# Other PSUM banks for the inputs of layer 2, and a layer norm that goes block by block

## The chip, the cores and the metric

The kernel runs on one core of one Trainium2 chip. Its time is the device time of the program in microseconds, the median of several executions. Five engines of the core work beside each other, each on its own list of instructions, in the order of that list: TensorE (PE) multiplies matrices into PSUM banks, VectorE (DVE) and GpSimd (POOL) do elementwise work, ScalarE (ACT) does functions, copies and squares, and SyncE (SP) issues the transfers. They wait for each other through semaphores only.

## The reference

Two pre-norm residual layers over 2048 positions of width 1024, and a final RMS norm. Layer 1 is gated linear attention. Layer 2, where the change lies, is a convolution module:

```
h = rmsnorm(x, norm_w[1])
a, gl, z = split(h @ w_in, 3)
u = a * sigmoid(gl)
u = causal depthwise convolution of u, 31 taps, + dw_b
u = silu(layernorm(u, ln_w, ln_b))
x = x + (u * silu(z)) @ w_out
out = rmsnorm(x, final_norm_w)
```

## The kernel before

Everything is kept transposed: channels on the 128 partitions, positions along the free dimension. The 2048 positions are worked in two halves of 1024 (`hf` 0 and 1), each of two blocks of 512 (`b` 0 and 1), and the 1024 channels in eight tiles of 128 (`k` or `c`). Each float32 factor of a product is written as a sum of a high and a low part of a shorter type (`ah`, `al` for activations, `wh`, `wl` for weights; `split` makes the first, ScalarE the high part, VectorE the difference), and a product is three matmuls, `ah*wh + al*wh + ah*wl`. A column of 128 outputs over one block is so 8 x 3 = 24 matmuls of 128x512 into one bank of the pool `mm`, which has three banks.

Layer 2 of a half has these parts. `prep_x1` loads the input from a scratch in memory (`t<-x_scratch`), multiplies it with the norm's weight and the factor 1/rms of its position, and splits it. `in2` runs the projections as a list of units: `glu` units give `u` (TensorE, a sigmoid on ScalarE, a product on VectorE), gate units give `silu(z)`, which goes to memory (`sz_scratch`). While TensorE runs them, `conv` does the 31 taps of a channel tile on VectorE, with some of the taps on ScalarE and GpSimd (`convA`), in three chains B, A and C that end in the tile `d`, and GpSimd adds all `d` into `S1`. `layernorm` takes the mean with matmuls of `S1` and a matrix of ones (the bank `pm`, L693), centres each `d` (L700), squares and sums, takes 1/rms (`v4n` on VectorE, a power `r` on GpSimd), spreads it over the partitions with matmuls of `ident` (`broadcast`), multiplies (L727), does the Silu with weight and bias (L728), and multiplies with the gate read back (`b<-b,d`, L729). The first half writes this `y` to memory, the second splits it. `out2` multiplies `y` with the last weights, adds the input (`u` or `d`, L838), sums squares (`acc`) and scales with the final norm.

The order on each engine is set when the kernel is built. The functions hand out their instructions in an order with priorities (`tc.high_priority`, above all for what TensorE needs, and with offset 1000 for mean and scale), a list of background work (`bg`) is fed in by a credit of estimated times (`pump`), and a scheduler of the framework places each instruction by its own estimate of when its operands and its buffers are free. So the number of buffers in a pool changes the order too. PSUM has eight banks: before, `mm` three, `b` two (the chains of the convolution and squares), `m` three (means, 1/rms, broadcasts).

Of the kernel before, what the change touches and what calls it, by code (L numbers as in the profile page):

```python
# [13 lines left out]
P = 128  # L14
# [3 lines left out]
NB = 512  # L18
# [22 lines left out]
def kernel(  # L41
# [23 lines left out]
    small = ctx.enter_context(tc.tile_pool(name="small", bufs=4))  # L65
    ps_mm = ctx.enter_context(tc.tile_pool(name="ps_mm", bufs=3, space=bass.MemoryType.PSUM))
    ps_b = ctx.enter_context(tc.tile_pool(name="ps_b", bufs=2, space=bass.MemoryType.PSUM))
    ps_m = ctx.enter_context(tc.tile_pool(name="ps_m", bufs=3, space=bass.MemoryType.PSUM))


    def mm_bank():
# [3 lines left out]
        return ps_b.tile([P, NB], F32, name="pb")  # L75

    def m_bank():
        return ps_m.tile([P, NB], F32, name="pm")


    def cc(base, j, n=1):
# [98 lines left out]
            pe.matmul(ps[:, j * P:(j + 1) * P], r4[:, j:j + 1].to_broadcast([P, P]), ident, start=True, stop=True)  # L180
        return ps

    def factor(q, dst):

        ps = broadcast(rt[:, q:q + 4])
        act.activation(dst, ps, AF.Copy)
        return dst

    def split(src):
        hi, lo = act_pair()  # L190
        act.activation(hi, src, AF.Copy)
        dve.tensor_tensor(lo, src, hi.bitcast(F32), ALU.subtract)  # L192
        return hi, lo

    def prep_x1(hf, b, rb, temp):
        a = []
        t0 = hf * TH + b * NB
        for k in range(KT):
            xr = temp()
            sp.dma_start(out=xr, in_=x1d[k * P:(k + 1) * P, t0:t0 + NB])  # L200
            dve.scalar_tensor_tensor(xr, xr, cc(C_NW2, k), rb, ALU.mult, ALU.mult)
            a.append(split(xr))
        return a

    def accumulate(acc, sq, first, eng):
# [3 lines left out]

    l1 = ExitStack()
    s2 = l1.enter_context(tc.tile_pool(name="s2", bufs=1))
    l1p = l1.enter_context(tc.tile_pool(name="l1p", bufs=1))
    l1c = l1.enter_context(tc.tile_pool(name="l1c", bufs=1))
# [329 lines left out]
    for hf in range(2):  # L545
        a, EEs, g3s = nxt
        stage = []
        for h in range(HEADS):
            EEs = head(hf, h, a, EEs, g3s, stage)
        nxt = ([], [], [])  # L550
        if hf == 0:
            out1(hf, stage, lambda: start_block(1, 0, *nxt))
        else:
            a = []
            rbs = [factor(4 * b, t2("E")) for b in range(2)]
            out1(hf, stage, lambda: a.append(prep_x1(0, 0, rbs[0], lambda: t2("raw"))))
            a.append(prep_x1(0, 1, rbs[1], lambda: t2("raw")))
    l1.close()


# [2 lines left out]
    l2 = ctx  # L563
    s2 = l2.enter_context(tc.tile_pool(name="s2b", bufs=4, reuse_waits="tile"))
    l2p = l2.enter_context(tc.tile_pool(name="l2p", bufs=1, reuse_waits="tile"))

    def t2():
        return s2.tile([P, NB], F32, name="t2")
# [110 lines left out]
    def layernorm(hf, dst, S1, y_out):  # L679

        st = {}

        def view(t, b):
            return t[:, :, b * 256:(b + 1) * 256]

        def wide(t):
            return t.rearrange("p (s t) -> p s t", s=2)

        def mean(b):
            def fn():  # L690
                with tc.high_priority(offset=1000):
                    ps = m_bank()
                    pe.matmul(wide(ps), ones, view(S1[0], b), start=True, stop=True)  # L693
                st["mu", b] = ps
            return fn

        def centre(b, k):
            def fn():
                d = view(dst[k], b)
                dve.scalar_tensor_tensor(d, wide(st["mu", b]), -1.0 / D, d, ALU.mult, ALU.add)  # L700
                add = dve if k % 2 == 0 or (hf == 1 and b == 0) else pool
                if k == 0:
                    sq = view(S1[0], b)
                else:
                    sq = wide(b_bank() if add is dve else b2())
                act.activation(sq, d, AF.Square)
                if k > 0:
                    S2 = view(S1[0], b)
                    add.tensor_tensor(S2, S2, sq, ALU.add)
            return fn  # L710

        def scale(b):
            def fn():
                v4, r4 = small.tile([P, 4], F32, name="v4n"), small.tile([P, 4], F32, name="r4")
                with tc.high_priority(offset=1000):
                    S2 = view(S1[0], b)
                    inv_rms([S2[:, p, j * P:(j + 1) * P] for p in range(2) for j in range(2)], v4, r4)
                    st["rb", b] = broadcast(r4)
            return fn

        def norm(b, k):
            def fn():
                z = b2()
                sp.dma_start(out=z, in_=szd[hf, k * P:(k + 1) * P, b * NB:(b + 1) * NB])
                zv = wide(z)
                d = view(dst[k], b)
                dve.tensor_tensor(d, d, wide(st["rb", b]), ALU.mult)  # L727
                act.activation(d, d, AF.Silu, scale=cc(C_LNW, k), bias=cc(C_LNB, k))  # L728
                (pool if hf == 0 or k % 2 == 1 else dve).tensor_tensor(zv, zv, d, ALU.mult)  # L729
                y_out(k, b, z)  # L730
            return fn

        means = [(0.0, mean(b)) for b in range(2)]
        centres = [[(0.6 if k % 2 else 0.0, centre(b, k)) for k in range(KT)] for b in range(2)]
        scales = [(0.7, scale(b)) for b in range(2)]
        norms = [[(0.6, norm(b, k), (hf, k, b)) for k in range(KT)] for b in range(2)]
        if hf == 0:
            return means + centres[0] + centres[1] + scales + norms[0] + norms[1]
        both = [t for pair in zip(centres[1], norms[0]) for t in pair]
        return means + centres[0] + scales[:1] + both + scales[1:] + norms[1]  # L740

    def in2(hf, sched, a, y_out, ahead):
        dst, S1 = [], []
# [30 lines left out]
        for i, group in enumerate(groups):  # L774
            last = i == len(groups) - 1
            units = []
            if last and hf == 0:
                for b in range(2):
                    rbs.append(factor(8 + 4 * b, acc_tile()))
            for kind, j in group:  # L780
                w = next_unit((16 if kind == "u" else 24) + j)
                u = None
# [21 lines left out]
    def out2(hf, a):  # L804
        for b in range(2):
# [22 lines left out]
            def project(u, w, s):  # L828
                ss = slice(s * n, (s + 1) * n)
                for c in range(2):  # L830
# [7 lines left out]
                        dve.tensor_tensor(xr, ps, xr, ALU.add)  # L838
                    with tc.high_priority(offset=PRIO):
                        acc = accs[s][:, 0:n]  # L840
                        sq = acc if ch == 0 else b_bank()[:, 0:n]
                        act.activation(sq, xr, AF.Square)
                        if ch > 0:
                            dve.tensor_tensor(acc, acc, sq, ALU.add)
                    pump(4.4 / ns, 0.0)

            def finish(s):
                ss = slice(s * n, (s + 1) * n)
                kp = () if ns == 1 else (1, 3, 5) if s else (1, 3, 5, 7)
                with tc.high_priority(offset=1000 if ns > 1 else 0):  # L850
                    v4, r4 = small.tile([P, 4], F32, name="v4"), small.tile([P, 4], F32, name="r4f")
                    inv_rms(columns(accs[s], n // P), v4, r4, b_bank)
                    rb = broadcast(r4[:, 0:n // P], b_bank)
                    if kp:
                        rbs = t2()[:, 0:n]
                        act.activation(rbs, rb, AF.Copy)
# [31 lines left out]
    def load_y(b):  # L888
        res = []
        for k in range(KT):  # L890
            raw = t2()
            sp.dma_start(out=raw, in_=yd[k * P:(k + 1) * P, b * NB:(b + 1) * NB])
            res.append(split(raw))
        return res

    rbs = []
    nxt = []

    def ahead_a():
        with tc.high_priority(offset=PRIO):  # L900
            nxt.append(prep_x1(1, 0, rbs[0], t2))

    in2(0, SCHED[0], a, y_spill, ahead_a)
    with tc.high_priority(offset=PRIO):
        nxt.append(prep_x1(1, 1, rbs[1], t2))
    a, nxt = nxt, []

    def ahead_b():
# [82 lines left out]
```

## Time and profile before

| | |
|---|---|
| times of three runs | 1647.65, 1643.82, 1647.19 us |
| median | 1647.19 us |
| profiled execution | 1651.64 us, its span 1649.5 us |
| TensorE busy | 1603.0 us, 97% |
| VectorE busy | 950.6 us, 58% |
| ScalarE busy | 739.7 us, 45% |
| GpSimd busy | 888.7 us, 54% |
| mean granted clock of TensorE | 0.99 of full speed |

Times in the rows count from the span's start. A group's line gives its busy time, the mean of one instruction, and the idle time of its engine ahead of it with what ended that (`<-`). A row of the timeline gives the start, the length, the engine, the line, the operation with the tiles it writes and reads, and how many such instructions lie in a row; the length is that of the whole row. Successive instructions of an engine overlap a little: a VectorE operation shown as 0.68 us starts 0.60 us after one like it. Layer 1 ends near 890 us, the place between the halves of layer 2 lies near 1140 to 1180, and `out2` begins near 1450.

### The profile page before, as it was taken

What the parts mean: (1) busy time and instruction counts of PE and PEld (TensorE: products, weight loads), DVE (VectorE), ACT (ScalarE), POOL (GpSimd) and SP (SyncE); (2) the same over time, 40 slices, a digit from 0 to 9 for tenths busy, and PEclk for the clock granted to TensorE, in tenths of its full rate; (3) what the DMA queues carried; (4) which work ended last, traced back from release to release, by engine and by line L of the source; (5) the groups of instructions that cost most, each with busy time, mean ns of one, the idle gap of its engine ahead of it and who ended that gap; (6) DMA issues with size and microseconds to landing.
All of it is one profiled execution on the core that took longest, in us unless ns stands there. A gap on an engine that the chain in (4) does not pass through costs nothing.

```text
span 1649.5 us, 23586 instructions
## 1 busy us (share of the span) xinstructions
PE 1603.0 (97%) x9028; PEld 1407.4 (85%) x9028; DVE 950.6 (58%) x1495; ACT 739.7 (45%) x1244; POOL 888.7 (54%) x789
## 2 busy tenths in 40 slices
PE   8999999999999999999999999999999999989897
PEld 6989999998889898989888888887788888878796
DVE  7433232251334232323425699998888999887753
ACT  6655353252447352523333354544473545435532
POOL 5353333234664434342344599976488988356552
PEclk9999999999999999999999999999999999999898
DMA  6021211144511212122454111224254122653743
GB/s 193 27 83 53 64 53 57 58 130 145 154 58 52 83 34 81 36 75 73 128 172 135 51 52 52 78 71 133 89 172 155 50 77 77 200 170 109 272 144 121
DMA packets 80160, 165.68 MB, mean 100 GB/s; under 512 B 7760, under 2 KB 22608, under 8 KB 80048
## 3 DMA queue, kind: packets, MB, share of 16 engines
q1 hardware_dynamic: 80048, 164.19, 31.1%
q8 instruction: 70, 1.15, 0.3%
q14 instruction: 42, 0.34, 0.1%
HBM read 128.51 MB, written 35.65 MB: 100 GB/s over the span
## 4 chain that ended last, share of the span: by engine, by line
PE 80%; DVE 5%; DMA 5%; ACT 4%; issue 3%; POOL 2%; SPq 0%; POOLq 0%; DVEq 0%; ACTq 0%
PE mm L146 70%; PE pb L146 3%; DMA wr<-in_wall_dram 2%; DVE al L192 2%; PE pb L390 1%; PE pb L392 1%; PE pm L381 1%; DVE pb L637 1%; DMA raw<-x_scratch 1%; POOL wl L127 1%; PE pm L416 1%; PE pm L290 1%; DVE d L727 1%; DMA t<-x_scratch 1%; POOL acc L207 1%
## 5 line engine op out<-in xcount | busy, mean ns | idle before, releaser
L146 PE MATMUL mm<-ah,wh 128*128 128x512 f32 (+1 forms) x1600 | 595.1, 387 | 21.1 <-DVE u L838 5.6
L146 PE MATMUL mm<-al,wh 128*128 128x512 f32 (+1 forms) x1600 | 592.3, 385 | 0.0
L146 PE MATMUL mm<-ah,wl 128*128 128x512 f32 (+1 forms) x1600 | 590.6, 385 | 0.2 <-POOL wl L127 0.2
L127 POOL TENSOR_TENSOR wl<-wr,wh 128x1024 fp32r<-128x1024 f32 x140 | 341.2, 2451 | 230.9 <-ACT wh L126 229.9
L146 PEld LDWEIGHTS mm<-ah,wh 128*128 128x128 f32 x1600 | 301.8, 190 | 83.1 <-DVE u L838 6.1
L146 PEld LDWEIGHTS mm<-ah,wl 128*128 128x128 f32 x1600 | 301.2, 190 | 57.8 <-POOL wl L127 0.7
L146 PEld LDWEIGHTS mm<-al,wh 128*128 128x128 f32 x1600 | 301.9, 190 | 57.1 <-issue 0.2
L146 PE MATMUL mm<-wh,ah 128*128 128x256 f32 x896 | 259.3, 289 | 0.0
L146 PE MATMUL mm<-wh,al 128*128 128x256 f32 x896 | 254.7, 284 | 0.0
L146 PE MATMUL mm<-wl,ah 128*128 128x256 f32 x896 | 254.2, 284 | 0.0
L625 POOL TENSOR_TENSOR convA<-convA,prod 128x512 f32<-128x512 f32 x158 | 207.0, 1312 | 11.6 <-ACT prod L623 4.9
L126 ACT ACTIVATE wh<-wr 128x1024 fp32r<-128x1024 f32 x144 | 145.5, 1051 | 145.7 <-PE mm L146 108.8
L637 DVE SCALAR_TENSOR_TENSOR pb<-u,C,pb 128x512 f32<-128x512 f32 x274 | 199.5, 747 | 1.0
L637 DVE SCALAR_TENSOR_TENSOR pb<-u,dwc,pb 128x512 f32<-128x512 f32 x240 | 178.2, 748 | 1.3
L146 PEld LDWEIGHTS mm<-wl,ah 128*128 128x128 f32 x896 | 171.5, 191 | 0.4
L146 PEld LDWEIGHTS mm<-wh,ah 128*128 128x128 f32 x896 | 171.3, 191 | 0.4
L146 PEld LDWEIGHTS mm<-wh,al 128*128 128x128 f32 x896 | 171.3, 191 | 0.0
L623 ACT ACTIVATE prod<-u,C 128x512 f32<-128x512 f32 x158 | 112.7, 721 | 105.0 <-POOL convA L625 104.6
L399 DVE SCALAR_TENSOR_TENSOR S<-S,dec,pb 128x256 f32<-128x256 f32 x56 | 26.8, 478 | 95.4 <-PE pb L146 95.3
L403 POOL TENSOR_TENSOR ss<-ss,e 128x1 f32<-128x1 f32 x64 | 13.3, 208 | 124.5 <-ACT g L402 124.5
L528 DVE TENSOR_TENSOR Q<-mm,Q 128x512 f32<-128x512 f32 x32 | 22.0, 688 | 92.6 <-PE mm L146 78.6
L443 DVE SCALAR_TENSOR_TENSOR vl<-mm,r,vh 128x256 fp32r<-128x256 f32 x48 | 22.9, 483 | 89.3 <-ACT vh L442 89.2
(191 smaller groups left out, 2078.3 us busy)
## 6 DMA issues: line engine op xcount, KB each, us to landing
wr<-in_wall_dram SPq DMA_DIRECT2D x144, 512.0 KB, 4.1
raw<-in_xT_dram SPq DMA_DIRECT2D x32, 256.0 KB, 3.7
Q<-in_xP_dram SPq DMA_DIRECT2D x32, 256.0 KB, 3.2
x_scratch<-Q SPq DMA_DIRECT2D x32, 256.0 KB, 3.2
sz_scratch<-t SPq DMA_DIRECT2D x32, 256.0 KB, 2.3
b<-sz_scratch SPq DMA_DIRECT2D x32, 256.0 KB, 3.0
g_scratch<-st SPq DMA_DIRECT2D x48, 128.0 KB, 1.9
raw<-g_scratch SPq DMA_DIRECT2D x24, 256.0 KB, 3.7
```

Of the source, the lines that this page charges most:

```text
L126: act.activation(wh[:, ks, :], raw, AF.Copy)
L127: (dve if i < 2 else pool).tensor_tensor(wl[:, ks, :], raw, wh[:, ks, :].bitcast(F32), ALU.subtract)
L146: pe.matmul(ps, s, m, start=(i == 0), stop=(i == 3 * n - 1))
L192: dve.tensor_tensor(lo, src, hi.bitcast(F32), ALU.subtract)
L207: eng.tensor_tensor(acc, acc, sq, ALU.add)
L290: pe.matmul(ps, wgs[:, k, :], m, start=(n == 0), stop=(n == 15))
L399: dve.scalar_tensor_tensor(S[h], S[h], dec[:, j:j + 1], kv, ALU.mult, ALU.add)
L443: dve.scalar_tensor_tensor(vl, ps, rr, vh.bitcast(F32), ALU.mult, ALU.subtract)
L528: dve.tensor_tensor(xr, ps, xr, ALU.add)
L623: act.activation(p, src, AF.Copy, scale=w)
L625: pool.tensor_tensor(acc, acc, p, ALU.add)
L637: dve.scalar_tensor_tensor(dstm, src, w, ps, ALU.mult, ALU.add)
```

## The change

Three things are changed, all for layer 2.

First, the input of layer 2 is no longer multiplied in place: the product goes to a PSUM bank, and both halves of the split read it there. The bank comes from `m` for the first half (while layer 1 still has its pools) and from the new pool `x` for the second. The factor 1/rms is read by the product straight from the bank of its broadcast, made inside `prep_x1`; the copies of it to SBUF (`factor`) are gone. The `y` of the second half is put together in an `x` bank as well, by VectorE alone, and split from there; and `y` of the first half, read back from memory, is copied by ScalarE to an `x` bank beside the high part, and VectorE's low part reads that copy.

Second, in layer 2 the three spare banks, `m` before, become one bank `m` and two banks `x`. The squares of centring and of `out2` take `x` in place of `b`; the mean and 1/rms of the second half take `b`, those of the first half `m`; the final norm's broadcast takes `m`.

Third, the layer norm's list is dealt out anew: mean 0, centrings 0, mean 1, centrings 1, then scale 0, norms 0, scale 1, norms 1 for the first half (before: both means, all centrings, both scales, all norms), and the first half's means and scales lose their offset of 1000.

```diff
@@ pools of layer 2
+    banks["m"] = l2.enter_context(tc.tile_pool(name="ps_n", bufs=1, space=bass.MemoryType.PSUM))
+    banks["x"] = l2.enter_context(tc.tile_pool(name="ps_x", bufs=2, space=bass.MemoryType.PSUM))
@@ prep_x1
-    def prep_x1(hf, b, rb, temp):
+    def prep_x1(hf, b, temp, rb_bank, bank):
         a = []
         t0 = hf * TH + b * NB
+        q = hf * 8 + b * 4
+        rb = broadcast(rt[:, q:q + 4], rb_bank)
         for k in range(KT):
             xr = temp()
             sp.dma_start(out=xr, in_=x1d[k * P:(k + 1) * P, t0:t0 + NB])
-            dve.scalar_tensor_tensor(xr, xr, cc(C_NW2, k), rb, ALU.mult, ALU.mult)
-            a.append(split(xr))
+            t = bank()
+            dve.scalar_tensor_tensor(t, xr, cc(C_NW2, k), rb, ALU.mult, ALU.mult)
+            a.append(split(t))
@@ layernorm
+        bank, ahead = (m_bank, 0) if hf == 0 else (b_bank, 1000)
@@ mean
-                with tc.high_priority(offset=1000):
-                    ps = m_bank()
+                with tc.high_priority(offset=ahead):
+                    ps = bank()
@@ centre
-                    sq = wide(b_bank() if add is dve else b2())
+                    sq = wide(x_bank() if add is dve else b2())
@@ scale
-                    inv_rms([S2[:, p, j * P:(j + 1) * P] for p in range(2) for j in range(2)], v4, r4)
-                    st["rb", b] = broadcast(r4)
+                    inv_rms([S2[:, p, j * P:(j + 1) * P] for p in range(2) for j in range(2)], v4, r4, bank)
+                    st["rb", b] = broadcast(r4, bank)
@@ norm
-                act.activation(d, d, AF.Silu, scale=cc(C_LNW, k), bias=cc(C_LNB, k))
-                (pool if hf == 0 or k % 2 == 1 else dve).tensor_tensor(zv, zv, d, ALU.mult)
-                y_out(k, b, z)
+                y = d if hf == 0 else wide(x_bank())
+                act.activation(y, d, AF.Silu, scale=cc(C_LNW, k), bias=cc(C_LNB, k))
+                if hf == 0:
+                    pool.tensor_tensor(zv, zv, d, ALU.mult)
+                    y_out(k, b, z)
+                else:
+                    dve.tensor_tensor(y, zv, y, ALU.mult)
+                    y_out(k, b, y.rearrange("p s t -> p (s t)"))
@@ the lists
         if hf == 0:
-            return means + centres[0] + centres[1] + scales + norms[0] + norms[1]
+            return (means[:1] + centres[0] + means[1:] + centres[1]
+                    + scales[:1] + norms[0] + scales[1:] + norms[1])
         both = [t for pair in zip(centres[1], norms[0]) for t in pair]
-        return means + centres[0] + scales[:1] + both + scales[1:] + norms[1]
+        return means[:1] + centres[0] + scales[:1] + means[1:] + both + scales[1:] + norms[1]
@@ out2
-                        sq = acc if ch == 0 else b_bank()[:, 0:n]
+                        sq = acc if ch == 0 else x_bank()[:, 0:n]
-                    inv_rms(columns(accs[s], n // P), v4, r4, b_bank)
-                    rb = broadcast(r4[:, 0:n // P], b_bank)
+                    inv_rms(columns(accs[s], n // P), v4, r4, x_bank)
+                    rb = broadcast(r4[:, 0:n // P], m_bank)
@@ load_y
-            res.append(split(raw))
+            hi, lo = act_pair()
+            x = x_bank()
+            act.activation(hi, raw, AF.Copy)
+            act.activation(x, raw, AF.Copy)
+            dve.tensor_tensor(lo, x, hi.bitcast(F32), ALU.subtract)
+            res.append((hi, lo))
@@ the second half's input
-            nxt.append(prep_x1(1, 0, rbs[0], t2))
+            nxt.append(prep_x1(1, 0, t2, m_bank, x_bank))
-        nxt.append(prep_x1(1, 1, rbs[1], t2))
+        nxt.append(prep_x1(1, 1, t2, m_bank, x_bank))
```

The order of the instructions moves most at the place between the halves. On TensorE before, both means of the first half (`pm<-S,ones`) stand together, behind the first 72 projection matmuls of the second half:

```order
L146 MATMUL mm<-ah,wh 128x512
L146 MATMUL mm<-al,wh 128x512
L146 MATMUL mm<-ah,wl 128x512
L693 MATMUL pm<-S_9658,ones 128x512 x2
L146 MATMUL mm<-ah,wh 128x512
```

On TensorE now, the two means (counted here as one row, each needs the one bank `pm`) and the broadcast of the second half's factor (`ident,rt`) stand ahead of the last gate column of the first half:

```order
L150 MATMUL mm<-al,wh 128x512
L150 MATMUL mm<-ah,wl 128x512
L696 MATMUL pm<-S_9677,ones 128x512 x2
L184 MATMUL pm<-ident,rt 128x128 x4
L150 MATMUL mm<-ah,wh 128x512
```

They have moved 96 projection matmuls to the front. Where the means stood before, with the same number of projection matmuls ahead, TensorE now has the square sum and the broadcast of 1/rms of block 1 and the broadcast of the factor for the input's block 1:

```order
L150 MATMUL mm<-al,wh 128x512
L150 MATMUL mm<-ah,wl 128x512
L172 MATMUL pm<-ones,S_9677 128x1 x4
L184 MATMUL pm<-ident,r_11239 128x128 x4
L184 MATMUL pm<-ident,rt 128x128 x4
L150 MATMUL mm<-ah,wh 128x512
```

All three write the one bank, one after the other. On VectorE before, the products and splits of the second half's input (`t<-t,C,acc`, `al<-t,ah`) lie between the last taps of convolution 7 (`pb<-u,dwc,pb`, ended by `d<-pb,dwb,convB`), and the centrings of both blocks follow in one row:

```order
L637 SCALAR_TENSOR_TENSOR pb<-u,dwc,pb 128x512 x10
L201 SCALAR_TENSOR_TENSOR t_11338<-t_11338,C,acc 128x512
L637 SCALAR_TENSOR_TENSOR pb<-u,dwc,pb 128x512
L201 SCALAR_TENSOR_TENSOR t_11345<-t_11345,C,acc 128x512
L201 SCALAR_TENSOR_TENSOR t_11352<-t_11352,C,acc 128x512
L637 SCALAR_TENSOR_TENSOR pb<-u,dwc,pb 128x512
L192 TENSOR_TENSOR al<-t_11338,ah 128x512
L192 TENSOR_TENSOR al<-t_11345,ah 128x512
```

On VectorE now, convolution 7 ends first, then come centrings 0, centrings 1, and only then the products into the banks `px` and their splits:

```order
L639 SCALAR_TENSOR_TENSOR pb<-u,dwc,pb 128x512 x15
L655 SCALAR_TENSOR_TENSOR d<-pb,dwb_96,convB 128x512
L703 SCALAR_TENSOR_TENSOR d<-pm,d 128x2x256 x8
L712 TENSOR_TENSOR S_9677<-S_9677,px 128x2x256 x2
L703 SCALAR_TENSOR_TENSOR d<-pm,d 128x2x256 x8
L712 TENSOR_TENSOR S_9677<-S_9677,px 128x2x256
L203 SCALAR_TENSOR_TENSOR px<-t_11032,C,pm 128x512
L203 SCALAR_TENSOR_TENSOR px<-t_11040,C,pm 128x512
L190 TENSOR_TENSOR al<-px,ah 128x512 x2
```

The input has moved behind the layer norm's centrings. On ScalarE now, five high parts stand ahead of a copy that empties an `mm` bank (`t<-mm`), and further on 16 Silus, five high parts and a table load stand ahead of the next ones:

```order
L189 ACTIVATE ah<-px 128x512 x5
L776 ACTIVATE t_11121<-mm 128x512
L189 ACTIVATE ah<-px 128x512
L776 ACTIVATE t_11223<-mm 128x512
L732 ACTIVATE d<-d,C 128x2x256 x16
L189 ACTIVATE ah<-px 128x512 x5
L759 ACT_TABLE_LOAD
L759 ACTIVATE t_11474<-mm 128x512
```

Before, all but one of the 16 high parts and the copies came ahead of the table load and of the squares, and the Silus later. On SP now, the fifth load of block 1's input (`t_11393<-x_scratch`) stands behind the stores of `y` and the loads of the gate tiles:

```order
L887 DMA y_scratch<-b_11264 128x512
L727 DMA b_11282<-sz_scratch 128x512
L887 DMA y_scratch<-b_11270 128x512
L727 DMA b_11316<-sz_scratch 128x512
L201 DMA t_11393<-x_scratch 128x512
```

`b_11264`, `b_11270` and `b_11316` are the eleventh, twelfth and fifteenth of the 16 gate tiles; four buffers hold them. Before, these loads came ahead of all of them.

## Rows read from the trace of the kernel before

**Rows 1.** The page, busy time of the engines, and VectorE's 40 slices
```profile
PE 1603.0 (97%) x9028; PEld 1407.4 (85%) x9028; DVE 950.6 (58%) x1495; ACT 739.7 (45%) x1244; POOL 888.7 (54%) x789
...
DVE  7433232251334232323425699998888999887753
```

**Rows 2.** Waits of PE: total us, times, longest us
```profile
PE mm L146 <- DVE u L838: 5.6, 2, 4.1
...
PE mm L146 <- ACT t L750: 4.0, 3, 1.8
PE pb L168 <- DVE acc L844: 3.7, 2, 2.6
```

**Rows 3.** Timeline of PE: start, length, form, count, idle before
```profile
1143.04 0.39 PE L146 MATMUL mm<-ah,wl 128*128 128x512 f32 x1
1146.12 0.50 PE L146 MATMUL mm<-ah,wh 128*128 128x512 f32 x1 [2.70 <-ACT t L767]
...
1171.70 1.98 PE L693 MATMUL pm<-S,ones 128*128 128x512 f32 x4 [1.88 <-POOL S L660]
1175.49 0.50 PE L146 MATMUL mm<-ah,wh 128*128 128x512 f32 x1 [1.80 <-ACT t L750]
```

**Rows 4.** Timeline of DVE at the end of convolution 7
```profile
1142.59 2.85 DVE L192 TENSOR_TENSOR al<-t,ah 128x512 fp32r<-128x512 f32 x1
...
1149.46 0.68 DVE L192 TENSOR_TENSOR al<-t,ah 128x512 fp32r<-128x512 f32 x1
...
1151.33 7.87 DVE L637 SCALAR_TENSOR_TENSOR pb<-u,dwc,pb 128x512 f32<-128x512 f32 x10
...
1168.10 0.74 DVE L653 SCALAR_TENSOR_TENSOR d<-pb,dwb,convB 128x512 f32<-128x512 f32 x1
...
1177.08 9.65 DVE L700 SCALAR_TENSOR_TENSOR d<-pm,d 128x512 f32<-128x512 f32 x16
```

**Rows 5.** Timeline of POOL, the sum of convolution 7 to the y products
```profile
1132.74 1.43 POOL L625 TENSOR_TENSOR convA<-convA,prod 128x512 f32<-128x512 f32 x1 [0.27 <-ACT prod L623]
...
1142.07 5.60 POOL L127 TENSOR_TENSOR wl<-wr,wh 128x1024 fp32r<-128x1024 f32 x2
...
1168.92 2.72 POOL L660 TENSOR_TENSOR S<-S,d 128x1024 f32<-128x1024 f32 x1 [1.71 <-DVE d L653]
...
1198.19 1.02 POOL L170 TENSOR_TENSOR r<-v4n,mhalf 128x4 f32<-128x4 f32 x1 [1.47 <-DVE v4n L169]
...
1211.61 5.07 POOL L729 TENSOR_TENSOR b<-b,d 128x512 f32<-128x512 f32 x4
...
1220.73 1.30 POOL L729 TENSOR_TENSOR b<-b,d 128x512 f32<-128x512 f32 x1 [0.27 <-DMA b<-sz_scratch]
...
1223.23 2.55 POOL L729 TENSOR_TENSOR b<-b,d 128x512 f32<-128x512 f32 x2
...
1229.75 1.30 POOL L729 TENSOR_TENSOR b<-b,d 128x512 f32<-128x512 f32 x1 [1.12 <-DMA b<-sz_scratch]
```

**Rows 6.** Timeline of ACT: a high part, a copy, a table load, Silus
```profile
1145.47 0.60 ACT L767 ACTIVATE t<-mm 128x512 f32<-128x512 f32 x1 [2.13 <-DVE al L192]
...
1149.58 0.63 ACT L191 ACTIVATE ah<-t 128x512 fp32r<-128x512 f32 x1 [0.68 <-DVE t L201]
...
1173.54 1.28 ACT L750 ACT_TABLE_LOAD   x1
...
1210.18 5.06 ACT L728 ACTIVATE d<-d,C 128x512 f32<-128x512 f32 x7
```

**Rows 7.** Groups of DVE by line, 1128 to 1176 us
```profile
L192 DVE TENSOR_TENSOR al<-t,ah 128x512 fp32r<-128x512 f32 x15 | 14.7, 1001 | 0.0
```

**Rows 8.** A window behind PE's stand at 1146.12: us, busy, granted clock
```profile
1147.30:1150.60 3.30, 3.30 (x10) 0.50 0.93 250
```

**Rows 9.** DMA issues: count, KB each, us to landing
```profile
t<-x_scratch SPq DMA_DIRECT2D x16, 256.0 KB, 3.7
y_scratch<-b SPq DMA_DIRECT2D x16, 256.0 KB, 3.6
```

More of the change, by code (lines that the diff above doesn't have):

```diff
@@ L67 @@
     ps_b = ctx.enter_context(tc.tile_pool(name="ps_b", bufs=2, space=bass.MemoryType.PSUM))
-    ps_m = ctx.enter_context(tc.tile_pool(name="ps_m", bufs=3, space=bass.MemoryType.PSUM))
+    l1 = ExitStack()
+    banks = {"m": l1.enter_context(tc.tile_pool(name="ps_m", bufs=3, space=bass.MemoryType.PSUM))}
     def mm_bank():
@@ L77, in m_bank, with x_bank @@
     def m_bank():
-        return ps_m.tile([P, NB], F32, name="pm")
+        return banks["m"].tile([P, NB], F32, name="pm")
+    def x_bank():
+        return banks["x"].tile([P, NB], F32, name="px")
     def cc(base, j, n=1):
@@ L181, in broadcast @@
         return ps
[L183 to L187, printed above, removed]
     def split(src):
@@ L207, in accumulate @@
             eng.tensor_tensor(acc, acc, sq, ALU.add)
-    l1 = ExitStack()
     s2 = l1.enter_context(tc.tile_pool(name="s2", bufs=1))
@@ L554 @@
             a = []
-            rbs = [factor(4 * b, t2("E")) for b in range(2)]
-            out1(hf, stage, lambda: a.append(prep_x1(0, 0, rbs[0], lambda: t2("raw"))))
-            a.append(prep_x1(0, 1, rbs[1], lambda: t2("raw")))
+            out1(hf, stage, lambda: a.append(prep_x1(0, 0, lambda: t2("raw"), b_bank, m_bank)))
+            a.append(prep_x1(0, 1, lambda: t2("raw"), b_bank, m_bank))
     l1.close()
@@ L714, in fn @@
                 v4, r4 = small.tile([P, 4], F32, name="v4n"), small.tile([P, 4], F32, name="r4")
-                with tc.high_priority(offset=1000):
+                with tc.high_priority(offset=ahead):
                     S2 = view(S1[0], b)
-                    inv_rms([S2[:, p, j * P:(j + 1) * P] for p in range(2) for j in range(2)], v4, r4)
-                    st["rb", b] = broadcast(r4)
+                    inv_rms([S2[:, p, j * P:(j + 1) * P] for p in range(2) for j in range(2)], v4, r4, bank)
+                    st["rb", b] = broadcast(r4, bank)
             return fn
@@ L776, in in2 @@
             units = []
-            if last and hf == 0:
-                for b in range(2):
-                    rbs.append(factor(8 + 4 * b, acc_tile()))
             for kind, j in group:
@@ L892, in load_y @@
             sp.dma_start(out=raw, in_=yd[k * P:(k + 1) * P, b * NB:(b + 1) * NB])
-            res.append(split(raw))
+            hi, lo = act_pair()
[4 more added lines that the diff above has]
+            res.append((hi, lo))
         return res
-    rbs = []
     nxt = []
```

## The prediction, on record before the changed kernel ran

> **What bounds the kernel now.** I read the busy shares first. TensorE is busy 1603.0 of 1649.5 us, and VectorE, at 58% overall, is at eight or nine tenths in 13 slices of the last half [rows 1]. So nothing can be gained but TensorE's waits, and anything that makes TensorE stand is paid in full. The waits come second: TensorE's table of them is short, and in layer 2 nothing in it lasts over 4.1 us at a time [rows 2]. The change touches the place between the two halves of layer 2, so the timeline of TensorE there comes third [rows 3]: a stand of 2.70 us that ends at 1146.12, one of 1.88 us ahead of the two mean sums at 1171.70, and one of 1.80 us that ends at 1175.49. Beside it stand the rows of VectorE [rows 4], GpSimd [rows 5] and ScalarE [rows 6]. VectorE there does three things mixed: the last taps of convolution 7, and the products and splits of the second half's input, of which 15 splits take 14.7 us [rows 7]. Both centrings follow in one run of 16 (9.65 us, 0.60 each), since the two means lie in two of three `m` banks.
>
> **What the edits do singly.** 64 splits now read PSUM in place of SBUF. A split costs 0.68 us where GpSimd is quiet (1149.46) and 2.85 where it lasts beside the 5.60 us pair of weight splits (1142.59) [rows 4, 5]. Priced at the gap between the mean of 14.7/15 = 0.98 and 0.68, that is about 0.3 x 64 = 19 us of VectorE's time. The Trainium skill ("SBUF — State Buffer", Who interferes with whom) says that a VectorE instruction with two SBUF inputs contends with a GpSimd instruction that reads SBUF. These two rows agree; by the rule alone every split gets cheaper and the change is a gain, which is the first rival below. The eight y products that leave GpSimd and become VectorE's free 8 x 1.3 = 10 us of GpSimd [rows 5]. The 16 extra copies on ScalarE (0.63 each [rows 6], 10 us) lie on an engine that is 45% busy [rows 1]. None of these engines bounds the whole, so I count all of it as nothing and look for what now makes TensorE wait.
>
> **Place between the halves, first stand.** In the changed order mean 0, mean 1 and the broadcast of 1/rms for the second half's block 0 stand ahead of the last gate column of the first half, not 96 matmuls later, and all three use the single `m` bank. TensorE gets there at about 1143.3 (the last matmul in front starts at 1143.04) [rows 3].
> - Convolution 7: its GpSimd sum is there at 1132.74 + 1.43 = 1134.2, or 1132.8 without VectorE's products beside it [rows 5]. Then three VectorE operations at 0.66 to 0.75, 16 taps at 7.87/10 = 0.79, and the closing one, 0.74 [rows 4]: 2.1 + 12.6 + 0.74. The end is 1148.3 to 1149.7, I take 1148.5. The products that lay between them are gone, so this ends 20 us earlier than before (1168.84).
> - GpSimd's sum 2.7 [rows 5], mean 0 half of 1.98 [rows 3]: 1152.2. Eight centrings at 0.60: 1157.0. Only then is the bank free. Mean 1: 1158. Two square sums on VectorE that alternate with GpSimd's: about 1159.6; eight centrings: 1164.4; broadcast: 1165.2.
> - The input now goes through two `x` banks: two products (0.66 each), two splits (0.68 long, 0.61 apart), 0.2 for ScalarE's high part between them: 2.75 a pair. ScalarE has five high parts (0.63) ahead of the copy (0.60) that empties the oldest `mm` bank; all three are full. 1165.2 + 5.5 + 0.66 + 0.63 + 0.60 gives 1172.6; I take 1173.
>
> TensorE resumes at 1173 where it did at 1146.1: +27. The Trainium skill ("PSUM — Partial Sum Buffer", Engine vs sequencer instructions) says that matmuls start and complete in program order. The stand before the means at 1171.70 agrees: the projection behind them needed neither. By the rule no ready column can pass the means, whatever the other engines save.
>
> **Second stand.** From 1173: 96 matmuls at 0.227 = 21.8 (the column pace between 1146.12 and 1169.8 is that plus a slow stretch), about 2.5 lost behind the stand (in before, after a stand of 2.7, the granted clock was 0.50, 1.2 GHz in place of 2.4, for 3.3 us [rows 8], which loses half of that; this stand is ten times as long), 1.5 for broadcasts and sums: 1198.8. Here the changed order has block 1's square sum, the broadcast of its 1/rms and that of the input's 1/rms in a row, each on the one bank, and only then the next column.
> - 1/rms 0 is there at about 1189; the first normed product and Silu (0.6 and 5.06/7 = 0.72 [rows 6]) make the first y product start at 1190.8. Seven y products stand ahead of the second 1/rms on GpSimd. In before the y tiles' four buffers let a round of four go every 9.1 us (1211.61, 1220.73, 1229.75), and the seventh ended 14.2 after the first began [rows 5]. So 1205, power 1.0 [rows 5], broadcast 0.5, eight norms as long as the centrings, 4.9: 1211.4; broadcast, five products, high part: 1218.7.
> - The fifth tile of block 1's input is loaded by SP behind the stores of y and the reload for the fifteenth product, which needs the eleventh stored. The eleventh ends 1190.8 + 18.2 + 3.9 = 1212.9; store 3.6, load 3.7 [rows 9], two issues 0.5: 1220.7; product and high part: 1222.
> - ScalarE has 16 Silus, five high parts and a table load (1.28 [rows 6]) ahead of the copy (0.60) that frees an `mm` bank. That gives 1220.6 by the first path, 1224 by the second, and 1215.5 if the y products ran back to back.
>
> I take 1222, nearest to the rows of the y rounds. Both orders have the same matmuls ahead here, and before resumed at 1175.49 [rows 3]: +46.5. A second slow stretch costs 2; the next stand in the old table (about 1.5, of the two that make up the other 2.2 of `t` L750 [rows 2]) should go: **+47**, bounds +40 and +52. VectorE idles or norms during both stands, so the gain of the splits is spent there.
>
> **The rest.** VectorE starts the second half's convolution some 27 us later and TensorE is 47 later, so VectorE, full there before, has about 20 us in hand: the stand behind `u` L838 (4.1 [rows 2]) goes, with 1.5 of slow clock, -5.6. Against it, block 1's mean comes later in the last part, and the y products of the second half and the squares of the output share the two `x` banks: the final square sum stands behind 16 norm steps. No row of before shows that; the bounds are 0 and +14 (eight output products of about 0.75, a store and a load of 3.6 and 3.7), and I take +6, the nearest row being the wait for `acc`, 2.6 [rows 2], at each of the two square sums, and a little for the reload behind. At the change of layers the single `m` bank doesn't exist yet: 0 to -1. Sum: about 0.
>
> **Sum.** 1651.6 for the profiled run + 47 + 0 = 1698.6. That run is 4.4 above the median of the runs shown (1647.2), so the forecast is **1694**. Its own range is 1680 (+40 and no cost in the last part) to 1708 (+52, +14 and the -5.6).
>
> **Rivals.**
> 1. *The splits win.* From PSUM they no longer clash with GpSimd, everything is early, and the waits of [rows 2, 3] go: 4.1 + 2.7 + 1.9 + 1.8 + 1.5 and about 1 elsewhere, with two slow stretches of 1.5, about -16: 1631. It needs mean 0 ready when TensorE gets there, 1143.3 - 3.7 = 1139.6 for convolution 7's end. Against it: its GpSimd sum is not there before 1132.8 and 15.4 us of VectorE's chain follow. If that chain could be overlapped with the columns the case decides; I see no way. 0.06.
> 2. *Only the first stand.* If y products don't hold the second 1/rms, and the copies of the first columns come between the Silus, the second stand is below the three `mm` banks' cover: +27 + 2.5 - 3.3: 1647 + 26 = 1673. For it: scratch loads may run ahead. Against it: ScalarE's program has the 16 Silus in one row. 0.17.
> 3. *The last part is dearer.* The shared `x` banks cost the full 14 (+8 on my value) and the stand at `u` L838 stays with its slow clock (+5.6): 1708. The short cover of the last columns speaks for it, VectorE's lead against it. 0.12.
> 4. *Nothing moves:* the banks freed in the first stand make good later all that was lost: 1647. 0.05.
>
> My forecast has 0.60. A difference under 0.3% (5 us) can't be told from none with this kernel. Slower: 0.60 + 0.17 + 0.12 = 0.89, less 0.01 for the edges: 0.88; same 0.05, faster 0.07. The range must take in rival 2 in part: 1662 to 1712.
>
> **What would show it.** In the new trace, three stands of TensorE in place of one: ahead of the mean, ahead of the last gate column ended by ScalarE's `t<-mm`, about 29 us in all from 1143; then 20 to 25 us from about 1199, ended by `t<-mm` behind a table load. The granted clock should be 0.5 for a few us behind each. VectorE's splits should have a mean near 0.68. The forecast is wrong if mean 1 doesn't wait for the eighth centring, if the second stand is under 10 us, or if the stand at `u` L838 (1453.67 before) is still there at 4 us.

## The result

| | before | changed |
|---|---|---|
| median | 1647.42 us (4 runs) | 1710.48 us (4 runs, 1708.33 to 1711.81) |
| ratio | | 1.038, 95% interval 1.0357 to 1.0402 |
| profiled execution, span | 1651.64, 1649.5 us | 1708.33, 1706.2 us |

The change makes the kernel slower by 63 us. The forecast was 1694 in 1662 to 1712; it falls 16 us short. The busy times of the changed kernel's page, to hold against [rows 1], are first:

```profile
PE 1611.2 (94%) x9028; PEld 1412.7 (83%) x9028; DVE 922.0 (54%) x1503; ACT 740.6 (43%) x1252; POOL 867.8 (51%) x781
...
PEclk9999999999999999999999999996699999999798
```

VectorE does 29 us less, GpSimd 21 us less, and TensorE 8 us more for the same matmuls (the slices of 6 to 8 tenths in its clock). What the splits were to gain is there, in the groups of VectorE by line of the changed kernel, 0.69 us each where they had a mean of about 1.0 [rows 7]:

```profile
L190 DVE TENSOR_TENSOR al<-px,ah 128x512 fp32r<-128x512 f32 x32 | 21.7, 689 | 1.7 <-ACT ah L189 1.1
...
L903 DVE TENSOR_TENSOR al<-px,ah 128x512 fp32r<-128x512 f32 x16 | 10.9, 685 | 4.7 <-ACT px L902 4.7
L190 DVE TENSOR_TENSOR al<-pm,ah 128x512 fp32r<-128x512 f32 x16 | 10.8, 687 | 1.5 <-ACT ah L189 1.5
```

But the waits of TensorE (total, times, longest), to hold against [rows 2], tell the rest:

```profile
PE mm L150 <- ACT t L759: 13.5, 3, 10.8
PE px L172 <- DVE acc L850: 11.6, 2, 6.9
PE mm L150 <- ACT t L776: 8.7, 3, 7.3
PE pm L696 <- POOL S L662: 8.0, 1, 8.0
...
PE pm L184 <- POOL r4f L174: 5.6, 3, 3.5
PE pm L184 <- DVE d L703: 5.4, 1, 5.4
PE pm L184 <- POOL r L174: 5.1, 1, 5.1
PE pm L184 <- DVE d L730: 5.1, 1, 5.1
PE pm L696 <- DVE d L703: 5.0, 1, 5.0
```

Seven of these nine stand ahead of sums and broadcasts (`pm`, `px`; those for `acc` and `r4f` lie in out2), the other two ahead of the columns behind them. TensorE's timeline between the halves has seven stands in a row (before: [rows 3]):

```profile
1152.84 2.08 PE L696 MATMUL pm<-S,ones 128*128 128x512 f32 x2 [8.00 <-POOL S L662]
1159.88 2.07 PE L696 MATMUL pm<-S,ones 128*128 128x512 f32 x2 [4.97 <-DVE d L703]
1167.39 2.08 PE L184 MATMUL pm<-ident,rt 128*128 128x128 f32 x8 [5.44 <-DVE d L703]
1176.78 0.79 PE L150 MATMUL mm<-ah,wh 128*128 128x512 f32 x1 [7.31 <-ACT t L776]
...
1208.86 2.08 PE L184 MATMUL pm<-ident,r 128*128 128x128 f32 x8 [5.14 <-POOL r L174]
1215.99 1.41 PE L184 MATMUL pm<-ident,rt 128*128 128x128 f32 x5 [5.05 <-DVE d L730]
1228.79 0.80 PE L150 MATMUL mm<-ah,wh 128*128 128x512 f32 x1 [10.76 <-ACT t L759]
```

The first four are the first stand, 25.7 us of idle time; the last three the second, 21.0 us (the view of the last row but one ends at 1217, with five of its eight matmuls). What holds them is seen on the other engines. On ScalarE the fifth high part of the new input comes just ahead of the copy that frees an `mm` bank and ends the first stand:

```profile
1175.64 0.60 ACT L189 ACTIVATE ah<-px 128x512 fp32r<-128x512 f32 x1 [1.42 <-DVE px L203]
1176.14 0.59 ACT L776 ACTIVATE t<-mm 128x512 f32<-128x512 f32 x1
```

For the second stand, on GpSimd (timeline, before: [rows 5]) seven products of y in rounds of four buffers, held by reloads, come ahead of the second power; on ScalarE (before: [rows 6]) Silus, five high parts and a table load come ahead of the copy that ends the second stand:

```profile
1195.32 5.07 POOL L734 TENSOR_TENSOR b<-b,d 128x512 f32<-128x512 f32 x4 [2.90 <-DMA t<-x_scratch]
1202.81 1.27 POOL L734 TENSOR_TENSOR b<-b,d 128x512 f32<-128x512 f32 x1 [2.43 <-DMA b<-sz_scratch]
...
1207.80 1.01 POOL L174 TENSOR_TENSOR r<-v4n,mhalf 128x4 f32<-128x4 f32 x1
```

```profile
1211.69 5.75 ACT L732 ACTIVATE d<-d,C 128x512 f32<-128x512 f32 x8 [11.57 <-DVE d L730]
...
1226.23 0.60 ACT L189 ACTIVATE ah<-px 128x512 fp32r<-128x512 f32 x1 [3.44 <-DVE px L203]
1226.85 1.28 ACT L759 ACT_TABLE_LOAD   x1
1228.14 0.60 ACT L759 ACTIVATE t<-mm 128x512 f32<-128x512 f32 x1
```

The fifth product of block 1's input, which that last high part needs, starts in VectorE's timeline only when its load has come:

```profile
1225.44 0.76 DVE L203 SCALAR_TENSOR_TENSOR px<-t,C,pm 128x512 f32<-128x512 f32 x1 [1.93 <-DMA t<-x_scratch]
```

The windows of TensorE (us, busy, granted clock) show the clock at its lower level (0.50, 1.2 GHz) during the two stands and behind them (before: [rows 8]); the last row is a third such stretch, in out2:

```profile
1147.60:1181.70 34.10, 11.15 (x24) 0.50 0.20 66
1181.80:1205.50 23.70, 21.92 (x110) 1.00 0.64 214
1205.70:1232.90 27.20, 8.23 (x26) 0.50 0.71 236
1598.20:1618.60 20.40, 10.45 (x34) 0.50 0.64 223
```

Most of the 61 us between the halves TensorE stood anyway; the lower clock cost at most half of the 19 busy us in them, part of that under the waits.

**Where the time goes.** The two kernels run the same 7872 projection matmuls, so the start of the Nth one in each trace can be compared. The table has the start in the trace of before, and by how much each later trace is behind it; e1 to e12 are the experiments below. Layer 2's second half begins at 5760, out2 at 6912. Out2 has four blocks of columns, two of the first half and then two of the second; the third begins at 7296, and at the 7368th its first three columns fill the three `mm` banks.

| N | before | changed | e1 | e2 | e3 | e4 | e5 | e6 | e7 | e8 | e9 | e10 | e11 | e12 |
|---|---|---|---|---|---|---|---|---|---|---|---|---|---|---|
| 5736 | 1146.1 | 30.7 | 25.5 | 1.3 | -3.3 | 0.4 | 31.1 | 32.0 | 0.7 | -0.5 | 0.8 | 29.7 | 1.9 | -1.5 |
| 5832 | 1175.5 | 53.3 | 37.1 | 2.2 | -1.0 | -7.3 | 53.6 | 28.6 | -6.9 | -8.1 | -6.8 | 41.5 | 1.2 | -0.4 |
| 6960 | 1437.8 | 48.7 | 32.9 | 4.0 | 0.3 | -7.4 | 49.7 | 24.5 | -7.1 | -8.3 | -7.0 | 36.8 | 2.9 | 2.9 |
| 7058 | 1466.6 | 44.1 | 28.5 | -1.6 | -3.7 | -12.8 | 45.4 | 21.4 | -13.6 | -14.5 | -12.5 | 37.0 | 2.8 | 2.7 |
| 7248 | 1514.0 | 50.5 | 35.0 | -2.2 | -0.7 | -7.9 | 51.3 | 27.3 | -10.4 | -9.9 | -6.9 | 38.9 | 2.8 | 2.2 |
| 7368 | 1553.7 | 59.3 | 41.4 | 22.9 | 11.2 | -1.2 | 56.4 | 37.6 | 5.5 | -3.7 | -10.7 | 31.1 | 9.8 | 18.1 |
| last | 1634.6 | 57.8 | 40.2 | 20.1 | 9.0 | -3.4 | 52.8 | 35.0 | 5.4 | -3.7 | -13.9 | 26.9 | 7.0 | 17.9 |

So the changed kernel loses 53 between the halves, wins 9 back up to the 7058th (half of it ahead of out2, half in its first columns, where the stand of 4 at `u` is gone), and loses 15 from there to the 7368th.

### The profile page after: what moved, and what is told of

Same layout as the page of the kernel before. It is cut to its first block, busy times and chain, and to the rows that moved or that the text cites. A ratio compares the mean times of both kernels' runs of the same rounds, so it can differ in the third digit from the quotient of the medians.

```text
span 1706.2 us, 23581 instructions
## 1 busy us (share of the span) xinstructions
PE 1611.2 (94%) x9028; PEld 1412.7 (83%) x9028; DVE 922.0 (54%) x1503; ACT 740.6 (43%) x1252; POOL 867.8 (51%) x781
## 4 chain that ended last, share of the span: by engine, by line
PE 84%; DVE 5%; ACT 4%; DMA 3%; POOL 2%; issue 2%; SPq 0%; POOLq 0%; DVEq 0%; ACTq 0%
PE mm L150 74%; PE pb L150 3%; PE pb L391 1%; PE pb L393 1%; DVE pb L639 1%; PE pm L382 1%; DMA raw<-in_xT_dram 1%; PE pm L417 1%; DVE d L703 1%; DMA wr<-in_wall_dram 1%; POOL acc L209 1%; DVE al L274 1%; POOL wl L131 1%; PE pm L291 1%; PE pm L184 1%
## 5 line engine op out<-in xcount | busy, mean ns | idle before, releaser
L150 PE MATMUL mm<-ah,wh 128*128 128x512 f32 (+1 forms) x1600 | 591.4, 386 | 29.7 <-ACT t L759 13.5
L444 DVE SCALAR_TENSOR_TENSOR vl<-mm,r,vh 128x256 fp32r<-128x256 f32 x48 | 22.9, 484 | 89.3 <-ACT vh L443 89.2
```

What stands on the lines that cost most here:

```text
L150: pe.matmul(ps, s, m, start=(i == 0), stop=(i == 3 * n - 1))
L444: dve.scalar_tensor_tensor(vl, ps, rr, vh.bitcast(F32), ALU.mult, ALU.subtract)
```

## The experiments

Theory A: the input of the second half now stands in the same rows of banks as the layer norm's tiles, banks are handed out in the order of the program, so the input comes after the layer norm, and TensorE waits for both. Theory B: one `m` bank is too few and its users queue.

**e1**, the three spare banks as one pool of three:
```
+    banks["m"] = l2.enter_context(tc.tile_pool(name="ps_n", bufs=3, ...))
+    banks["x"] = banks["m"]          # and x_bank's tiles take the name "pm"
```


> The changed kernel, with its three spare banks of layer 2 in one pool of three that means, factors, input products and squares all take in turn. Theory A (the input of the second half waits in the same row of banks as the layer norm's tiles, so it comes after the layer norm and TensorE stands for it): the input stays behind, only the wait of mean 1 for the centrings of block 0 goes (5 us, and perhaps as much at the broadcast), so 1695 to 1708 us, with the two stands between the halves still over 30 us together. Theory B (one bank for means and factors is too few, so they queue for it): the queue is gone, the place between the halves costs under 10 us more than before, 1655 to 1668 us in all.

1692.32 us, ratio 1.0257 (1.0232 to 1.0282). A, a little under its range: with three banks to choose from the input is nearly as late, both stands are there (24.1 and 12.2 us). B falls: the queue for one bank costs some 16 us of the 53, not the rest.

**e2**, the input as before:
```
-            t = bank()
+            t = xr if hf == 1 else bank()     # factors copied to SBUF early, as before
```


> The changed kernel with the second half's input prepared as before (factor copied early to SBUF, product in place, split from SBUF); one m bank, two x banks and the new order of the layer norm stay. Theory A: the input is early again, the place between the halves is within 6 us of before, and only what out2 lost stays (about +9): 1650 to 1662 us. Theory B: the means still queue for one bank ahead of a column, so at least the first stand stays (25 us): 1675 to 1690 us.

1671.31 us, 1.0131 (1.011 to 1.0153), outside both ranges. Between the halves A is right (2.2 at 5832). But between the 7248th and the 7368th it now loses 25 us, where the changed kernel loses 9. In the table of waits of e2:

```profile
PE px L172 <- DVE acc L858: 26.4, 2, 19.9
```

So the changed kernel has a second loss. That it is in part hidden there behind the first, because out2 begins more than 40 us later and other engines have time to run ahead, is likely and not shown.

**e3**, the kernel before with one `m` bank in layer 2:
```
+    banks["m"] = l2.enter_context(tc.tile_pool(name="ps_n", bufs=1, ...))
```


> The kernel before with one m bank in layer 2 in place of three and nothing else changed. Theory A: within 8 us of before, 1642 to 1655 us, since the input does not use that bank in the critical stretch. Theory B: the means and factors queue, at least +20: 1667 us or more.

1660.62 us, 1.0065 (1.0048 to 1.0083), between the ranges. Between the halves nothing is lost (-1.0), against B; the 12 us go in out2, between 7248 and 7368, which neither theory had.

**e4**, both ties cut:
```
-        rb = broadcast(rt[:, q:q + 4], rb_bank)
+        rb = rb_bank if hf == 1 else broadcast(...)   # hf 1: early copy in SBUF
...
-                    sq = wide(x_bank() if add is dve else b2())
+                    sq = wide(b_bank() if add is dve else b2())   # same in out2
```


> The changed kernel with both ties between the input and the layer norm cut: the factors are copied to SBUF early as before, and the squares of centring and of out2 take b banks again, so that the two x banks hold only products of inputs and y. The splits still read PSUM. Theory A: the place between the halves is within 6 us of before, out2 loses less than in the changed kernel, and the stand behind u is gone: 1636 to 1652 us. Theory B: one m bank still queues, 1670 us or more.

The square sum of the final norm goes from `x` to `b` with the squares, in e4 and in e5. 1646.11 us, 0.9982 (0.9971 to 0.9992), as A had it. The splits still read PSUM, and the place between the halves is now 7 us faster than before.

**e5**, only the squares moved (second edit of e4):
```
-                    sq = wide(x_bank() if add is dve else b2())
+                    sq = wide(b_bank() if add is dve else b2())   # same in out2
```


> The changed kernel with only the squares (of centring and of out2) back in b banks; the factor of the input is still broadcast inside prep_x1 into the one m bank, behind the means. Theory A (either tie alone, by the m bank or by the x banks, is enough to put the input behind the layer norm): the place between the halves stays at +40 or more against the kernel before, 1680 to 1700 us. Rival C (the squares in the x banks are the tie that matters): like e4, 1646 to 1655 us.

1702.85 us, 1.0339 (1.0312 to 1.0367), just over A's range; 53.6 at 5832. C falls.

**e6**, only the factor moved (first edit of e4):
```
-        rb = broadcast(rt[:, q:q + 4], rb_bank)
+        rb = rb_bank if hf == 1 else broadcast(...)   # hf 1: early copy in SBUF
```


> The changed kernel with only the factors copied to SBUF early as before; the squares still take the x banks in which the input's products lie. Theory A: the input stays behind the layer norm by the x banks, +25 or more between the halves and out2 dear as in e2 or the changed kernel, 1680 to 1705 us. Rival D (the broadcast in the m bank is the tie that matters): the place is repaired and only out2's loss stays, 1660 to 1675 us.

1686.03 us, 1.0237 (1.021 to 1.0265): A. The first stand is as long (32.0 at 5736), though its last two waits are now for the square sum and the 1/rms of block 0; the second is nearly gone. Either tie is enough for the first; only both cut remove it.

**e10**, the other way round: the kernel before, with three `m` banks, and one edit:
```
-            dve.scalar_tensor_tensor(xr, xr, cc(C_NW2, k), rb, ALU.mult, ALU.mult)
-            a.append(split(xr))
+            t = m_bank()
+            dve.scalar_tensor_tensor(t, xr, cc(C_NW2, k), rb, ALU.mult, ALU.mult)
+            a.append(split(t))
```


> The kernel before with one edit: the input's product goes to an m bank (three of them, as before) and both splits read it there. Theory A: the three banks go round in program order, the layer norm's means and sums are handed out ahead of the input, so the input comes after them; the stand between the halves returns without any of the other edits: 1668 to 1690 us. Theory B (banks are too few only when there is one): no loss, 1642 to 1652 us.

1677.08 us, 1.0188 (1.0167 to 1.021): A. Its table of waits has the changed kernel's stands, for which no other edit was needed; e4 keeps the new list and the lower priority of the means, and has none of them:

```profile
PE mm L146 <- ACT t L768: 15.4, 3, 14.0
PE mm L146 <- ACT t L751: 14.4, 2, 13.7
PE pm L694 <- POOL S L661: 10.4, 2, 9.3
```

**e7**, e4 with the last part as before (`means` of the second half at once in the `x` banks, 1/rms in `m`, final norm in `b`, y in SBUF with half of its products on GpSimd):
```
-                    ps = bank()
+                    ps = bank() if hf == 0 else x_bank()
...
-                rb = broadcast(r4[:, 0:n // P], m_bank)
+                rb = broadcast(r4[:, 0:n // P], b_bank)
```


> e4 with the last part as before: both means of the second half at once in the two x banks (free there), 1/rms in m, the final norm in b, y in SBUF with half of its products on GpSimd. e4 was 12.8 us ahead of the kernel before when out2 began and gave 11.6 back by the end of block 0. Theory A (banks and the late mean 1 take it back): most of the 12.8 is kept, 1633 to 1641 us. Rival E (out2 has its own pace, set by its loads and by VectorE, so an early start only waits): 1643 to 1648 us.

1656.57 us, 1.0051 (1.0033 to 1.007). Both missed: ahead by 13.6 at 7058, behind by 5.5 at 7368.

**e8**, e7 with y in `x` banks, put together by VectorE alone:
```
+                y = d if hf == 0 else wide(x_bank())      # as in the changed kernel
```


> e7, but y of the second half in x banks, by VectorE alone, as in the changed kernel. Theory A: the banks are free there and y in PSUM costs nothing, within 3 us of e7: 1633 to 1643 us. Rival F (the eight more products on VectorE and the two banks that each y holds until it is split are what out2 pays for): 6 to 12 us over e7, 1640 to 1650 us.

1646.16 us, 0.9993 (0.998 to 1.0005). F had the wrong sign: y in PSUM, with all its products on VectorE, gains 10 us there. A missed its range too.

**e9**, e8 with the final norm's 1/rms at high priority in the three blocks that didn't have it (the expectation speaks of the first alone):
```
-                with tc.high_priority(offset=1000 if ns > 1 else 0):
+                with tc.high_priority(offset=1000):
```


> e8 with 1/rms of the final norm and its broadcast for block 0 of out2 at the high priority that block 1 has, so that TensorE takes them near its 7220th and 7260th projection matmul and not at the 7360th. e8 was 14.5 us ahead of the kernel before when out2 began and lost 12 until the last evacuation of block 0's u tiles (a stand of 9.7 us). Theory A2 (the late final norm of block 0 holds the u tiles that block 1 needs): that stand shrinks to under 3 us and 1634 to 1641 us remain. Rival E (out2 has its own pace by VectorE's sum of work): the eight products of the final norm now delay the layer norm instead, 1643 to 1650 us.

1638.11 us, 0.994 (0.9925 to 0.9955): faster than both kernels, as A2 had it. The timeline of VectorE has the products of the first block's norm. The `u` tiles that they free are loaded again for out2's third block (the second half's block 0), whose columns can't leave their `mm` banks before. Here is the row of the kernel before, of the changed one, of e8 and of e9:

```profile
1535.08 4.03 DVE L864 SCALAR_TENSOR_TENSOR u<-u,C,pb 128x512 f32<-128x512 f32 x6
```
```profile
1603.40 4.03 DVE L870 SCALAR_TENSOR_TENSOR u<-u,C,pm 128x512 f32<-128x512 f32 x6
```
```profile
1540.34 4.04 DVE L878 SCALAR_TENSOR_TENSOR u<-u,C,pb 128x512 f32<-128x512 f32 x6 [0.70 <-PE pb L184]
```
```profile
1510.61 1.39 DVE L878 SCALAR_TENSOR_TENSOR u<-u,C,pb 128x512 f32<-128x512 f32 x2
```

TensorE starts the 7368th matmul 18.6 us after the first of them in the kernel before (with a stand of 1.6), 9.6 after in the changed one and 9.7 in e8, where it stands 9.7: store, load and evacuation take that long. In e9 they come 32 us ahead and that stand is gone. The norms of the other two blocks come earlier in e9 as well, but the 10 us that e9 wins on e8 lie between the 7248th and the 7368th, and in e8 those two come only from the 7512th on. In the changed kernel the evacuation into `u` waits for the load:

```profile
1612.27 1.29 DVE L844 TENSOR_TENSOR u<-mm,u 128x512 f32<-128x512 f32 x2 [2.92 <-DMA u<-x_scratch]
```

**e11**, the kernel before with y of the second half in `m` banks, put together by VectorE alone, and **e12**, with only the new list:
```
+                y = d if hf == 0 else wide(m_bank())      # e11
```
```
+            return (means[:1] + centres[0] + means[1:] + centres[1]
+                    + scales[:1] + norms[0] + scales[1:] + norms[1])   # e12, and hf 1 alike
```


> The kernel before with one edit: y of the second half put together in an m bank by VectorE alone and split from there. From e7 against e8 (y in SBUF 10 us dearer there) theory A: out2 gains, 1638 to 1644 us. Rival G (the gain of e8 over e7 was that block 0's final norm lay badly in e7, not y): no difference, 1645 to 1650 us, or a loss of up to 5 us where the final norm of block 0 comes later.

> The kernel before with only the layer norm's list dealt out block by block (three m banks, input and y as before). All theories: the means stay behind the 72nd projection matmul of the second half and the order of the other engines hardly moves, within 4 us of before, 1643 to 1651 us.

e11: 1655.82 us, 1.0048 (1.0032 to 1.0064); e12: 1665.18 us, 1.0102 (1.0076 to 1.0128). Both are slower than any theory had them, and both lose it between 7248 and 7368; between the halves neither loses more than 2 us, so the new list alone does not make the two stands. In the program order of TensorE the broadcast of the first block's final 1/rms (eight matmuls) lies at the 7298th projection matmul in the kernel before, at the 7368th in the changed kernel, e1, e2, e4 to e8, e11 and e12, and in e3 with two matmuls at the 7310th and six at the 7368th. It lies at the 7258th in e9 and between the 7250th and the 7262nd in e10. These two are the only ones that win on the kernel before between 7248 and 7368; the other eleven lose 5 to 25 us there. e12's wait behind it:

```profile
PE mm L146 <- DVE u L839: 22.5, 2, 19.3
```

That this late norm is the cause is shown for e8 by e9. In the changed kernel, e1, e2 and e4 to e7 the 7368th matmul starts 9.6 to 9.8 us behind the first product of that norm, as in e8, so the same chain ends the stand there. For e3, e11 and e12 (15 to 17 us) it is argued from place and order, and in e11 TensorE's stand is one of 14.1 ahead of a square sum. e7 is 10 us slower than e8 because that product starts 9.2 us later (1549.55 against 1540.34); 3.6 of it are two stands behind weight parts that e8 doesn't have, and the rest stays open.

## Why the prediction came out as it did

**What bounds the kernel**: held. TensorE alone decides; 29 us less on VectorE and 21 less on GpSimd bought nothing.

**First stand**: held, 4 us late. Resumption forecast at 1173, measured 1176.78; mean 0 forecast at 1151.2 and started at 1152.84, mean 1 at 1157.0 against 1159.88, the broadcast 1164.4 against 1167.39. Convolution 7 ended at 1150.4, 0.7 over its range.

**Second stand**: held, with its two paths, and 7 us late. Forecast 1222, where the later path alone gave 1224; measured 1228.79. The y rounds began at 1195.32, not 1190.8, since 1/rms 0 came 4 us late; rounds and load then ran nearly as forecast, and the fifth product came at 1225.44 against 1220.7. At 5832 the loss is 53.3, just outside the bounds of +40 to +52. That +48.7 remained at the 6960th, near the forecast +47, is partly luck: 4.6 came back where the sum had a loss of 0.5. Of these, 2.2 are two stands of the kernel before (1.53 and 0.69) that are gone; the rest was not traced.

**The cause behind the order** was not in the prediction. It named the single bank, and by e1 that is some 16 us. What moved the input was that it shares banks with the layer norm: e10 has the stand with three banks, e4 has none of it with one.

**The rest** is the term that was mis-sized: taken as 0, measured +9. The -5.6 for the stand at `u` was right (48.7 to 43 by the 7080th). The cost of out2 was taken as +6 of 0 to +14 and was 14.9 (42.9 at the 7080th to 57.8 at the last). Of this, 7.6 lie between the 7080th and the 7248th, with a stand for banks whose columns wait to be added to `d`; the kernel before has that stand too, but later, behind the 7248th. Their lines in the tables of waits, of the changed kernel and of the one before:

```profile
PE mm L150 <- DVE d L844: 4.4, 2, 4.2
```
```profile
PE mm L146 <- DVE d L838: 4.5, 2, 4.1
```

So that stand is moved and not added. What is added lies at the 7368th: 14.7 us of stands against 1.6 before. The mechanism named, squares waiting for the `x` banks, is worth about 6 (from 7248 to the last matmul the changed kernel loses 7.3, and e5, without it, 1.5). The larger part, some 9 us, is in e5 too, where TensorE stands 11.4 at the 7368th. It goes with the final norm of the first block, which is handed out late, and that was not seen. The timeline of the changed kernel has the last two of its stands there:

```profile
1609.40 1.87 PE L172 MATMUL px<-ones,acc 128*128 128x1 f32 x8 [6.86 <-DVE acc L850]
1613.01 0.79 PE L150 MATMUL mm<-ah,wh 128*128 128x512 f32 x1 [1.74 <-DVE u L844]
```

**The sum**: of the 16 us that are missing, about 9 are this term, 2 the place between the halves, and the others lie in the profiled runs, which stand 57 us apart where the medians stand 63.

**Rivals**: the splits did get cheaper (0.69 us each); in the change this was covered by the stands. e4, with these splits, is 7 to 13 us ahead of the kernel before from the 5832nd to the 7058th, and e2, with the second half's input split from SBUF, is 2 behind at 5832. But e4 also moved the squares, so no run gives the share of the splits alone. The third rival's full 14 in out2 came true, its stand at `u` did not.

**The two rules.** By the Trainium skill ("SBUF — State Buffer", Who interferes with whom), splits with one SBUF input should not slow down beside GpSimd. The trace agrees: the 32 splits that read `px` through L190 took 0.68 to 0.69 us each, where the 32 from SBUF in the kernel before (`al<-t`) took 0.67 to 2.85. By the Trainium skill ("PSUM — Partial Sum Buffer", Engine vs sequencer instructions), no matmul passes another. Nothing in the traces speaks against it, but they don't show a ready column held up. Of the 46.7 us, TensorE stood 28.6 ahead of sums and broadcasts and 18.1 ahead of the column itself, whose `mm` bank came free only by the copy at 1176.14, or at 1228.14. So both stands end with ScalarE's copy behind the high parts of the late input; the broadcast of the input's factor (`ident,rt`) is a link of that chain, since the products wait for it. The stand at 1171.70, from which the prediction reads the rule, is no better proof: the column behind it then waited for a bank until 1175.49.

## What to carry to other kernels

A pool of buffers is a queue in program order: a tile that is put into the pool of another stage waits for that stage, and on an engine that runs in order everything behind it waits too. Before spare banks are dealt out anew, see who else takes from each pool, and in the new order whether matmuls for sums and broadcasts have come ahead of columns, and whether the copies that empty the columns' banks have come behind work that waits for another pool. When a large loss is repaired, a second one behind it shows: measure the parts from both sides.

## What was not expected of the hardware

The clock of TensorE stayed at 0.50 during the stands themselves, 34.1 and 27.2 us, and rose 5 us after the first and 4 us after the second ended, though in between single matmuls of the layer norm ran; a short stand of 2.7 us in the kernel before was followed by 3.3 us of it [rows 8]. A split with its operand in PSUM took 0.69 us, about as long as one from SBUF where GpSimd was quiet (0.68 [rows 4]).
